# Where a gated ConvFFN convolves its five plain up-projection blocks

## The chip, the cores and the metric

The kernel runs on one core of a Trainium2 chip. The metric is device time in microseconds of one execution of the whole program. TensorE (PE) multiplies, ScalarE (ACT) and VectorE (DVE) do the elementwise work, GpSimd (POOL) helps with a few additions, and every DMA is issued by SyncE (SP), on one queue and in the order in which the program wrote it.

## The reference

One decoder layer over 2048 tokens of 1024 features: a token mixer, then the channel mixer that matters here. `causal_dwconv` is a three-tap convolution over positions with a bias, one set of taps for each of the 5632 features; the two features left of a position may come from the chunk before it.

```python
h = rms_norm(x, ln2_g[l]) * (1.0 + sc2) + sh2
u = jnp.einsum('bsd,df->bsf', h, w_up[l])
u = causal_dwconv(u, conv_w[l], conv_b[l])
a, v = jnp.split(u, 2, axis=-1)
x = x + gt2 * jnp.einsum('bsf,fd->bsd', jax.nn.silu(a) * v, w_down[l])
```

## The kernel before

The tokens are cut into four chunks of 512. Chunks 2p and 2p+1 form pass p, and each of the two passes runs the mixer for both chunks and then the FFN (`plan_ffn`). In the FFN the first chunk is called the first half (`m` = 0) and the second one the second half (`m` = 1). Every fp32 product is three matmuls over a high and a low part of both operands, so each weight and each activation is split: a cast on ACT gives the high part, a subtraction on DVE the low one (lines 129 and 132).

The up-projection has 22 blocks f of 128 gate features and 128 value features. Seventeen of them (5 to 21) go through a Strassen scheme over both halves at once, seven steps each (`strassen`). The first five are "plain": `plain(f, 0)` for f = 0 to 4 runs ahead of the Strassen blocks, while DVE and ACT build the operands of the scheme (`build("T1")` to `build("T4")`, `weights_first`), and `plain(f, 1)` for f = 0 to 4 runs behind them, just ahead of the down-projection. A plain block is 48 matmuls: 24 for the gate features, which fill one PSUM bank, and 24 for the value features, which fill another.

`conv_unit` (L1125 to L1144) takes a plain block's two banks. For each it scales on ACT (L1130), adds the two earlier taps on DVE (L1131, L1132), mends the first two columns from `halo` (L1134, L1135) and keeps the last two columns in it (L1136). Then come the Silu on ACT (L1139), the gate product on DVE (L1140) and, noted in `stores`, the write of that half of A[f] to DRAM. With `m` = 1 the first half of A[f] is read back (`fore`, L1151), since `diff_a` and `diff_b` need both halves for the operands of the down-projection.

A Strassen block does the same over 1024 columns: `open_ct` puts the halo ahead of them, `tap_act` (L1272) scales on ACT, `tap_vec` (L1280, L1281) adds two taps on DVE, `silu` (L1284) and `gate` (L1290) end it.

What sets the order: ACT and SP run in the program's order throughout. In the plain blocks DVE, PE and POOL are ordered by a planner; in the Strassen steps all five are in the program's order. `flush()` at the start of a block or step issues the stores that were noted before it, and a store waits on SP for the engine that makes its data. The weights of `plain(f, 1)` come back from DRAM as high and low parts (`w_load`, L1839), 2 MB a block, into four pairs of buffers and, while `big_pairs[0]` is 2, into two further pairs taken from the pool `big`, as soon as a block before has released them. `w_load()` stands at the end of a step, behind the step's own DMAs.

The down-projection is made of units of 18 or 15 matmuls. `unit(u)` issues the load of the weights of unit u+4, splits those of unit u+2 (`prep_w`, on ACT and DVE) and multiplies. Units 0 and 1 are split at the start of `plain(4, 1)`, ahead of its own work; the loads of units 0 to 3 stand there too.

Of the kernel before, what the change touches and what calls it, by code (L numbers as in the profile page):

```python
# [9 lines left out]
F32 = mybir.dt.float32  # L10
F32R = mybir.dt.float32r
U8 = mybir.dt.uint8
AF = mybir.ActivationFunctionType
# [4 lines left out]
P = 128  # L18
S = 2048
D = 1024  # L20
# [43 lines left out]
def kernel(  # L64
# [41 lines left out]
    def slot(dt=F32):  # L106
        return slots.tile([P, T], dt, tag="s", name="s")
# [238 lines left out]
    def at(i, fn):  # L346
        side[i].append(fn)
# [14 lines left out]
    def feature_mm(h, dst):  # L362
        def mm(w):
            pt = bank()
            n = 0
            for k in range(KD):
                if k == KD // 2:
                    run_half()
                for wv, hv in split_passes(w[0], h[k]):
                    pe.matmul(  # L370
                        pt, lhsT=wv[:, k * P : (k + 1) * P], rhs=hv, start=(n == 0), stop=(n == 3 * KD - 1)
                    )
                    n += 1
            dst.append(pt)

        return mm
# [140 lines left out]
    x1_d = [[dram.tile([P, D], F32, name=f"x1d{s}_{k}") for k in range(4)] for s in range(NSUB)]  # L517
    acts_d = [[dram.tile([P, D], F32, name=f"actd{i}_{f}") for f in range(NF)] for i in range(2)]
    T_d = [[[dram.tile([P, T], F32, name=f"td{i}_{t}_{p}") for p in range(NF // 2)] for t in range(4)] for i in range(2)]
    h12_d = [[dram.tile([P, T], F32, name=f"h12d{i}_{k}") for k in range(4)] for i in range(2)]  # L520

    def x1_of(s, j):
        return x1[s][j % 4][:, (j // 4) * T : (j // 4 + 1) * T]
# [583 lines left out]
    def plan_ffn(sg):  # L1107
# [11 lines left out]
        def taps(idx):  # L1119
            return [cw_sb[:, idx, j : j + 1] for j in range(3)]  # L1120

        fore = {}


        def conv_unit(f, m, pa, pv):  # L1125
            res = []
            for idx, pt in ((f, pa), (NF + f, pv)):
                t_ = slot()
                w0, w1, w2 = taps(idx)
                act.activation(t_, pt, AF.Identity, scale=w2, bias=cb_sb[:, idx : idx + 1])  # L1130
                vec.scalar_tensor_tensor(t_[:, 1:T], pt[:, 0 : T - 1], w1, t_[:, 1:T], op0=ALU.mult, op1=ALU.add)  # L1131
                vec.scalar_tensor_tensor(t_[:, 2:T], pt[:, 0 : T - 2], w0, t_[:, 2:T], op0=ALU.mult, op1=ALU.add)  # L1132
                hl = halo[:, idx, :]
                vec.scalar_tensor_tensor(t_[:, 0:1], hl[:, 1:2], w1, t_[:, 0:1], op0=ALU.mult, op1=ALU.add)  # L1134
                vec.scalar_tensor_tensor(t_[:, 0:2], hl, w0, t_[:, 0:2], op0=ALU.mult, op1=ALU.add)  # L1135
                vec.tensor_copy(hl, pt[:, T - 2 : T])  # L1136
                res.append(t_)
            ta, tv = res
            act.activation(ta, ta, AF.Silu)  # L1139
            vec.tensor_tensor(ta, ta, tv, op=ALU.mult)  # L1140
            stores.append((A[f][:, m * T : (m + 1) * T], ta))
            if m:
                made[f] = fore.pop(f), ta, tv

        def plain(f, m):
            def mm(w):
                flush()
                if m:
                    load_partner(f)
                    fore[f] = slot()  # L1150
                    sp.dma_start(fore[f], A[f][:, 0:T])  # L1151
                    for g in list(made):
                        diff_a(g)
                        diff_b(g)
                pts = []
                for wi in range(2):
                    feature_mm(h1T[(s0, s1)[m]], pts)([w[wi]])
                    while between:
                        between.pop()()
                conv_unit(f, m, *pts)  # L1160

            return mm


        def build(name):
            s0k = [x1_of(s0, k) for k in range(4)]
            spare = vec if sg else pool
            if name == "T1":
                h12 = [norm2_f32(s1, k) for k in range(4)]
                for k in range(4):  # L1170
                    sp.dma_start(h12_d[sg][k], h12[k])
                for k in range(4):
                    vec.tensor_tensor(s0k[k], h12[k], s0k[k], op=ALU.subtract)
                src = s0k
            elif name == "22":
                src = [norm2_f32(s1, k + 4) for k in range(4)]
            elif name == "T2":
                for k in range(4):
                    vec.tensor_tensor(s0k[k], x1_of(s1, k + 4), s0k[k], op=ALU.subtract)
                src = s0k  # L1180
            elif name == "T3":
                src = [x1_of(s1, k) for k in range(4)]
                for k in range(4):
                    spare.tensor_tensor(src[k], x1_of(s1, k + 4), src[k], op=ALU.subtract)
            else:
                src = [x1_of(s0, k + 4) for k in range(4)]
                for k in range(4):
                    spare.tensor_tensor(src[k], src[k], s0k[k], op=ALU.subtract)
            for k in range(4):
                B[name].append(parts_of(src[k]))  # L1190
            if name == "T4":
                B["11"] = [h1T[s0][k] for k in range(4)]
                B["21"] = [h1T[s0][k + 4] for k in range(4)]
                del x1[s0], x1[s1]
# [67 lines left out]
        def open_ct(f, c):  # L1262
            ct[c, f] = big()
            act.copy(ct[c, f][:, 0:2], halo[:, f + c * NF, :])

        def save_halo(f, c):
            act.copy(halo[:, f + c * NF, :], ct[c, f][:, D : D + 2])

        def tap_act(f, c):
            idx = f + c * NF  # L1270
            cvt[c, f] = big()
            act.activation(  # L1272
                cvt[c, f][:, 0:D], ct[c, f][:, 2 : 2 + D], AF.Identity, scale=taps(idx)[2], bias=cb_sb[:, idx : idx + 1]
            )

        def tap_vec(f, c):
            t_ = cvt[c, f][:, 0:D]
            src = ct.pop((c, f))
            w0, w1, _ = taps(f + c * NF)
            vec.scalar_tensor_tensor(t_, src[:, 1 : 1 + D], w1, t_, op0=ALU.mult, op1=ALU.add)  # L1280
            vec.scalar_tensor_tensor(t_, src[:, 0:D], w0, t_, op0=ALU.mult, op1=ALU.add)  # L1281

        def silu(f):
            act.activation(cvt[0, f][:, 0:D], cvt[0, f][:, 0:D], AF.Silu)  # L1284
# [3 lines left out]
        def gate(f):  # L1288
            a, v = cvt.pop((0, f))[:, 0:D], cvt.pop((1, f))[:, 0:D]
            vec.tensor_tensor(a, a, v, op=ALU.mult)  # L1290
            stores.append((A[f], a))
            made[f] = a[:, 0:T], a[:, T:D], v[:, 0:T]
# [199 lines left out]
            strassen(f, near(-1), near(1), near(2), near(-2))  # L1492
        add([], lambda: last_block(SF[-1]), "own")
        i1 = len(steps)
        for f in range(FILL):
            add([f"ua{f}", f"uv{f}"], plain(f, 1))

# [584 lines left out]
```

## Time and profile before

| | us |
|---|---|
| median of 3 runs | 2350.69 |
| lowest, highest | 2350.02, 2354.12 |
| profiled execution, its own time | 2356.09 |
| its span, first to last instruction | 2354.0 |
| TensorE busy in the span | 2291.7 |

All rows come from the profiled execution. Times are counted from the start of its span. A name such as `s<-ps` tells what an instruction writes and reads, and L1130 is line 1130 of the kernel. What stands in brackets with an arrow is the idle time of the engine ahead of an instruction and what ended it.

### The profile page before, as it was taken

How to read it: one execution, taken by the hardware profiler on the slowest of the kernel's cores; microseconds unless marked ns; L12 is line 12 of the kernel's file. 1: busy time of each engine (PE TensorE's matmuls, PEld its weight loads, DVE VectorE, ACT ScalarE, POOL GpSimd, SP SyncE). 2: the span in 40 equal slices, each digit the busy share in tenths (PEclk: the TensorE clock that was granted, in tenths of full speed). 3: DMA queues.
4: the chain of work that ended last, by engine and by line, in shares of the span. 5: the costliest groups of instructions: out<-in, count | busy, mean ns of one | idle time of the engine just before them, and what ended most of it. 6: DMA issues, size and time to landing. Idle time of an engine off the chain costs nothing. (4 is left out here: it accounts for less than half of the span.)

```text
span 2354.0 us, 32995 instructions
## 1 busy us (share of the span) xinstructions
PE 2291.7 (97%) x12310; PEld 1904.2 (81%) x12310; DVE 1672.2 (71%) x2641; ACT 1050.9 (45%) x1957; POOL 333.0 (14%) x320
## 2 busy tenths in 40 slices
PE   8999999998999999999999999999999999999996
PEld 6878788886888888788778888888888888888885
DVE  6677646658887788777894474446487788877778
ACT  5643433245555554443544242323455554535453
POOL 3342224112000000100134212320100000000001
PEclk9999999999999999999999999999999999999998
DMA  9866684647322237996664446344632223599751
GB/s 349 339 228 220 250 324 171 216 179 268 117 103 95 102 120 260 372 361 229 201 256 170 180 162 234 144 180 144 237 118 97 99 94 113 202 372 371 254 185 72
DMA packets 192639, 481.75 MB, mean 205 GB/s; under 512 B 21288, under 2 KB 36056, under 8 KB 192480
## 3 DMA queue, kind: packets, MB, share of 16 engines
q1 hardware_dynamic: 192480, 479.66, 56.6%
q8 instruction: 96, 1.57, 0.3%
q14 instruction: 63, 0.52, 0.1%
HBM read 366.20 MB, written 113.38 MB: 204 GB/s over the span
## 5 line engine op out<-in xcount | busy, mean ns | idle before, releaser
L1235 PE MATMUL ps<-s,whi 128*128 128x512 f32 x1904 | 586.2, 389 | 1.0 <-ACT whi L1224 1.0
L1235 PEld LDWEIGHTS ps<-s,whi 128*128 128x128 f32 x1904 | 357.2, 188 | 76.1 <-ACT whi L1224 1.4
L1567 PE MATMUL ps<-s,whi 128*128 128x512 f32 (+1 forms) x1272 | 386.8, 386 | 6.3 <-ACT whi L129 3.3
L1235 PE MATMUL ps<-s,wlo 128*128 128x512 f32 x952 | 369.8, 389 | 0.0
L370 PE MATMUL ps<-s,whi 128*128 128x512 f32 x1040 | 325.5, 395 | 10.8 <-ACT whi L129 10.8
L462 POOL TENSOR_TENSOR s<-s 128x512 f32<-128x512 f32 (+1 forms) x69 | 96.7, 1402 | 1490.3 <-ACT s L461 955.9
L1567 PEld LDWEIGHTS ps<-s,whi 128*128 128x128 f32 x1272 | 239.3, 190 | 55.9 <-DVE s L132 4.7
L858 PE MATMUL ps<-whi,s 128*128 128x512 f32 (+1 forms) x992 | 252.6, 345 | 0.0
L1567 PE MATMUL ps<-s,wlo 128*128 128x512 f32 (+1 forms) x636 | 245.4, 387 | 4.9 <-DVE wlo L132 4.9
L370 PEld LDWEIGHTS ps<-s,whi 128*128 128x128 f32 x1040 | 194.4, 189 | 53.3 <-ACT whi L129 12.0
L132 DVE TENSOR_TENSOR wlo<-big,whi 128x768 fp32r<-128x768 f32 (+3 forms) x152 | 161.8, 1070 | 73.7 <-ACT whi L129 71.8
L1235 PEld LDWEIGHTS ps<-s,wlo 128*128 128x128 f32 x952 | 178.7, 188 | 36.9
L370 PE MATMUL ps<-s,wlo 128*128 128x512 f32 x520 | 203.4, 392 | 1.5 <-DVE wlo L132 1.5
L370 PE MATMUL ps<-s,big 128*128 128x512 f32 x792 | 185.6, 391 | 0.0
L858 PEld LDWEIGHTS ps<-whi,s 128*128 128x128 f32 x992 | 165.2, 189 | 20.9 <-issue 0.4
L129 ACT CAST whi<-big 128x768 fp32r<-128x768 f32 (+3 forms) x160 | 134.5, 848 | 106.5 <-DVE big L1548 26.3
L370 PEld LDWEIGHTS ps<-s,big 128*128 128x128 f32 x792 | 147.8, 188 | 31.7 <-issue 1.3
L858 PE MATMUL ps<-wlo,s 128*128 128x512 f32 (+2 forms) x496 | 150.3, 341 | 3.1 <-DVE wlo L132 3.1
L1228 DVE TENSOR_TENSOR wlo<-big,whi 128x1024 fp32r<-128x1024 f32 (+1 forms) x136 | 145.4, 1085 | 5.9 <-ACT whi L1224 5.7
L1224 ACT CAST whi<-big 128x1024 fp32r<-128x1024 f32 (+1 forms) x136 | 127.6, 940 | 41.4 <-DVE big L1212 41.4
L1567 PEld LDWEIGHTS ps<-s,wlo 128*128 128x128 f32 x636 | 120.9, 190 | 29.9 <-DVE wlo L132 6.7
L1280 DVE SCALAR_TENSOR_TENSOR big<-big,cw_sb 128x1024 f32<-128x1024 f32 x68 | 87.4, 1285 | 68.2 <-ACT big L1272 68.2
(228 smaller groups left out, 3652.1 us busy)
## 6 DMA issues: line engine op xcount, KB each, us to landing
big<-in_wt SPq DMA_DIRECT2D x104, 512.0 KB, 3.3
s<-td SPq DMA_DIRECT2D x110, 256.0 KB, 5.1
big<-in_wd SPq DMA_DIRECT2D x72, 384.0 KB, 6.3
s<-actd SPq DMA_DIRECT2D x98, 256.0 KB, 5.3
s<-in_w_ada SPq DMA_DIRECT2D x96, 256.0 KB, 6.0
big<-in_wd SPq DMA_DIRECT2D x72, 320.0 KB, 4.2
actd<-big SPq DMA_DIRECT2D x34, 512.0 KB, 2.6
td<-s SPq DMA_DIRECT2D x54, 256.0 KB, 5.5
```

The source lines that it names most:

```text
L129: act.copy(hi, src)
L132: (lo_engine or vec).tensor_tensor(lo, src, hi.bitcast(F32), op=ALU.subtract)
L370: pe.matmul(pt, lhsT=wv[:, k * P : (k + 1) * P], rhs=hv, start=(n == 0), stop=(n == 3 * KD - 1))
L462: engine.tensor_tensor(acc, acc, sq, op=ALU.add)
L858: pe.matmul(pt[:, 0 : c1 - c0], lhsT=hv[:, tt * P : (tt + 1) * P], rhs=wv[:, k2 * stride + c0 : k2 * stride + c1], start=(m == 0), stop=(m ...
L1224: act.copy(dst[f][0][:, 0:n], src[f][:, 0:n])
L1228: vec.tensor_tensor(lo[:, 0:n], src[f][:, 0:n], hi[:, 0:n].bitcast(F32), op=ALU.subtract)
L1235: pe.matmul(pt, lhsT=wv[:, c0 : c0 + P], rhs=hv, start=(start and n == 0), stop=(n == 11), skip_group_check=not start)
L1280: vec.scalar_tensor_tensor(t_, src[:, 1 : 1 + D], w1, t_, op0=ALU.mult, op1=ALU.add)
L1567: pe.matmul(pt[:, cols], lhsT=wv[:, ki * P : (ki + 1) * P], rhs=hv[:, cols], start=(start and n == 0), stop=(n == 3 * np_ - 1), skip_group ...
```

## The change

With `m` = 0 a plain block no longer convolves. Its two banks are copied on ACT to two buffers, and these raw products are stored to DRAM (`raw_d`, 256 KB each). With `m` = 1 the two raw halves are read back into the left halves of two `ct` buffers, the new products are copied beside them, and the block is convolved over 1024 columns with the Strassen blocks' own helpers. One store then writes all of A[f], 512 KB, and `fore` is gone.

Two smaller edits go with it. In pass 0 the eight subtractions of `build("T3")` and `build("T4")` move from POOL to DVE, where pass 1 already had them. And `big_pairs[0]` is set to 0 at the start of the second half's plain blocks, so that no further weight pair goes into the pool `big`.

```diff
@@ -517,6 +517,7 @@
     x1_d = [[dram.tile([P, D], F32, name=f"x1d{s}_{k}") for k in range(4)] for s in range(NSUB)]
     acts_d = [[dram.tile([P, D], F32, name=f"actd{i}_{f}") for f in range(NF)] for i in range(2)]
     T_d = [[[dram.tile([P, T], F32, name=f"td{i}_{t}_{p}") for p in range(NF // 2)] for t in range(4)] for i in range(2)]
+    raw_d = [[[dram.tile([P, T], F32, name=f"rawd{i}_{f}_{c}") for c in range(2)] for f in range(FILL)] for i in range(2)]
     h12_d = [[dram.tile([P, T], F32, name=f"h12d{i}_{k}") for k in range(4)] for i in range(2)]
 
     def x1_of(s, j):
@@ -1119,52 +1120,42 @@
         def taps(idx):
             return [cw_sb[:, idx, j : j + 1] for j in range(3)]
 
-        fore = {}
-
-
-        def conv_unit(f, m, pa, pv):
-            res = []
-            for idx, pt in ((f, pa), (NF + f, pv)):
-                t_ = slot()
-                w0, w1, w2 = taps(idx)
-                act.activation(t_, pt, AF.Identity, scale=w2, bias=cb_sb[:, idx : idx + 1])
-                vec.scalar_tensor_tensor(t_[:, 1:T], pt[:, 0 : T - 1], w1, t_[:, 1:T], op0=ALU.mult, op1=ALU.add)
-                vec.scalar_tensor_tensor(t_[:, 2:T], pt[:, 0 : T - 2], w0, t_[:, 2:T], op0=ALU.mult, op1=ALU.add)
-                hl = halo[:, idx, :]
-                vec.scalar_tensor_tensor(t_[:, 0:1], hl[:, 1:2], w1, t_[:, 0:1], op0=ALU.mult, op1=ALU.add)
-                vec.scalar_tensor_tensor(t_[:, 0:2], hl, w0, t_[:, 0:2], op0=ALU.mult, op1=ALU.add)
-                vec.tensor_copy(hl, pt[:, T - 2 : T])
-                res.append(t_)
-            ta, tv = res
-            act.activation(ta, ta, AF.Silu)
-            vec.tensor_tensor(ta, ta, tv, op=ALU.mult)
-            stores.append((A[f][:, m * T : (m + 1) * T], ta))
-            if m:
-                made[f] = fore.pop(f), ta, tv
 
         def plain(f, m):
             def mm(w):
                 flush()
                 if m:
                     load_partner(f)
-                    fore[f] = slot()
-                    sp.dma_start(fore[f], A[f][:, 0:T])
+                    for c in range(2):
+                        open_ct(f, c)
+                        sp.dma_start(ct[c, f][:, 2 : 2 + T], raw_d[sg][f][c])
                     for g in list(made):
                         diff_a(g)
                         diff_b(g)
-                pts = []
-                for wi in range(2):
-                    feature_mm(h1T[(s0, s1)[m]], pts)([w[wi]])
+                for c in range(2):
+                    pts = []
+                    feature_mm(h1T[(s0, s1)[m]], pts)([w[c]])
                     while between:
                         between.pop()()
-                conv_unit(f, m, *pts)
+                    if m == 0:
+                        t_ = slot()
+                        act.copy(t_, pts[0])
+                        stores.append((raw_d[sg][f][c], t_))
+                        continue
+                    act.copy(ct[c, f][:, 2 + T : 2 + D], pts[0])
+                    tap_act(f, c)
+                    save_halo(f, c)
+                    tap_vec(f, c)
+                    if c == 0:
+                        silu(f)
+                    else:
+                        gate(f)
 
             return mm
 
 
         def build(name):
             s0k = [x1_of(s0, k) for k in range(4)]
-            spare = vec if sg else pool
             if name == "T1":
                 h12 = [norm2_f32(s1, k) for k in range(4)]
                 for k in range(4):
@@ -1181,11 +1172,11 @@
             elif name == "T3":
                 src = [x1_of(s1, k) for k in range(4)]
                 for k in range(4):
-                    spare.tensor_tensor(src[k], x1_of(s1, k + 4), src[k], op=ALU.subtract)
+                    vec.tensor_tensor(src[k], x1_of(s1, k + 4), src[k], op=ALU.subtract)
             else:
                 src = [x1_of(s0, k + 4) for k in range(4)]
                 for k in range(4):
-                    spare.tensor_tensor(src[k], src[k], s0k[k], op=ALU.subtract)
+                    vec.tensor_tensor(src[k], src[k], s0k[k], op=ALU.subtract)
             for k in range(4):
                 B[name].append(parts_of(src[k]))
             if name == "T4":
@@ -1492,6 +1483,7 @@
             strassen(f, near(-1), near(1), near(2), near(-2))
         add([], lambda: last_block(SF[-1]), "own")
         i1 = len(steps)
+        at(i1, lambda: big_pairs.__setitem__(0, 0))
         for f in range(FILL):
             add([f"ua{f}", f"uv{f}"], plain(f, 1))
 
```

## Rows read from the trace of the kernel before

**Rows 1.** Page, busy time: us, share of the span, instructions of each engine.

```profile
PE 2291.7 (97%) x12310; PEld 1904.2 (81%) x12310; DVE 1672.2 (71%) x2641; ACT 1050.9 (45%) x1957; POOL 333.0 (14%) x320
```

**Rows 2.** Busy time by stretch (from:to length, busy each, PEclk, DMA): the plain blocks.

```profile
core 0: us, PE busy (x) PEld busy (x) DVE busy (x) ACT busy (x) POOL busy (x), PEclk, DMA share, GB/s
536.60:603.70 67.10, 57.27 (x240) 46.56 (x239) 61.25 (x97) 40.11 (x58) 14.17 (x8) 0.90 0.72 264
1682.70:1738.10 55.40, 54.39 (x241) 44.69 (x239) 48.80 (x98) 33.07 (x51) 0.00 (x0) 1.00 0.55 187
927.50:982.00 54.50, 54.39 (x240) 44.70 (x239) 39.20 (x72) 19.64 (x31) 10.07 (x7) 1.00 1.00 366
2062.30:2116.70 54.40, 54.40 (x242) 45.05 (x241) 39.18 (x77) 16.90 (x26) 0.00 (x0) 1.00 1.00 368
```

**Rows 3.** Timeline (start, length, instruction) of PE: the gap in pass 0's first half.

```profile
589.60 2.17 PE L370 MATMUL ps<-s,whi 128*128 128x512 f32 x4 [9.83 <-ACT whi L129]
```

**Rows 4.** Timeline of ACT ahead of that matmul.

```profile
579.44 1.44 ACT L1130 ACTIVATE s<-ps,cb_sb,cw_sb 128x512 f32<-128x512 f32 x2
587.99 0.63 ACT L1139 ACTIVATE s<-s 128x512 f32<-128x512 f32 x1 [7.10 <-DVE s L1135]
588.52 1.03 ACT L129 CAST whi<-big 128x1024 fp32r<-128x1024 f32 x1
```

**Rows 5.** Views of lines 1179 and 1184: ns min/median/max, first and last start.

```profile
L1179 DVE TENSOR_TENSOR big<-big x8: 684/1230/1782, 570.3 to 1714.6; 128x512 f32<-128x512 f32 x8
L1184 DVE TENSOR_TENSOR big<-big x4: 683/685/686, 1715.8 to 1719.4; 128x512 f32<-128x512 f32 x4
```

**Rows 6.** Groups by shape: count, busy us, mean ns | idle time before, releasers.

```profile
L1131 DVE SCALAR_TENSOR_TENSOR s<-ps,cw_sb,s 128x511 f32<-128x511 f32 x40 | 29.8, 745 | 7.2 <-ACT s L1130 7.2
L1338 ACT COPY big<-ps 128x512 f32<-128x512 f32 x34 | 19.9, 586 | 22.1 <-PE ps L1235 22.1
L1272 ACT ACTIVATE big<-big,cb_sb,cw_sb 128x1024 f32<-128x1024 f32 x68 | 84.6, 1245 | 5.0 <-DVE big L1332 3.8
L1280 DVE SCALAR_TENSOR_TENSOR big<-big,cw_sb 128x1024 f32<-128x1024 f32 x68 | 87.4, 1285 | 68.2 <-ACT big L1272 68.2
L1284 ACT ACTIVATE big<-big 128x1024 f32<-128x1024 f32 x34 | 36.1, 1062 | 23.5 <-DVE big L1281 23.5
L1290 DVE TENSOR_TENSOR big<-big 128x1024 f32<-128x1024 f32 x34 | 41.5, 1219 | 0.0
```

**Rows 7.** Waits of SP's queue: us in total, times, longest.

```profile
SPq L1117 <- DVE big L1290: 246.6, 30, 10.7
```

**Rows 8.** Timeline of SP in pass 1's first second-half block.

```profile
2071.59 0.32 SPq L1117 DMA_DIRECT2D actd<-big  x1
...
2073.70 0.45 SPq L1151 DMA_DIRECT2D s<-actd  x1
```

**Rows 9.** View of line 1151: its ten DMAs from issue to landing.

```profile
DMA to landing us min/median/max: 4.6/5.9/7.1
```

**Rows 10.** The same row for all DMAs of tile actd.

```profile
DMA to landing us min/median/max: 2.0/5.1/9.5
```

**Rows 11.** Timelines of PE, ACT and DVE where pass 1's down-projection starts.

```profile
2116.45 0.62 PE L1567 MATMUL ps<-s,whi 128*128 128x512 f32 x2
...
2118.04 1.28 ACT L119 ACT_TABLE_LOAD   x1
2119.34 0.84 ACT L129 CAST whi<-big 128x768 fp32r<-128x768 f32 x1
...
2120.20 0.96 DVE L132 TENSOR_TENSOR wlo<-big,whi 128x768 fp32r<-128x768 f32 x1
```

**Rows 12.** Timelines of DVE and PE in pass 0's second half.

```profile
949.33 0.69 DVE L1312 TENSOR_TENSOR s<-s 128x512 f32<-128x512 f32 x1 [5.16 <-DMA s<-actd]
...
983.93 0.73 PE L1567 MATMUL ps<-s,whi 128*128 128x512 f32 x2 [2.04 <-ACT whi L129]
```

**Rows 13.** Page, DMA issues: count, KB each, median us to landing.

```profile
big<-in_wd SPq DMA_DIRECT2D x72, 384.0 KB, 6.3
```

## The prediction, made before the change was run

> **What bounds the kernel now.** The page's first part comes first: TensorE is busy for 2291.7 us of a span of 2354.0 [rows 1]. The change removes no matmul, so all it can win is idle PE time, 62 us in the whole kernel, and only what of it lies in the plain blocks. The busy times by stretch show that [rows 2]. Five plain blocks are 240 matmuls. In both second halves, and in pass 1's first half but for one microsecond, PE is busy throughout, and 240 matmuls take 54.4 us: 10.9 us a block, 0.227 us a matmul. In pass 0's first half they take 67.1 us, 12.7 more, at a granted clock of 0.90. The PE timeline says where: one gap of 9.83 us, ended by a cast on ACT [rows 3]; the other 2.9 us are the slow clock behind it (the lower of the two levels, 1.2 GHz). The ACT timeline gives the cause [rows 4]: the cast of the next block's weights stands in program order behind the Silu of a convolution, and the Silu waited 7.10 us for DVE. DVE is busy for 61.25 of the 67.1 us [rows 2]. The second halves are the opposite: DVE is busy for 39 of 54 us, but the DMA engines have a share of 1.00 at 366 to 368 GB/s [rows 2]. So the change takes work from a stretch bound by DVE and ACT's order, and puts work, loads and stores into one bound by the DMA queue.
>
> **First halves: the gain.** Each block loses four taps of 0.745 us on DVE, 3.0 us, and its halo columns and gate product besides [rows 6]: over 15 us a pass. ACT gets two copies of 0.586 us [rows 6] and no Silu, so nothing on it waits for a convolution. The eight subtractions moved in pass 0 add 8 x 0.685 = 5.5 us to DVE [rows 5]; but DVE's own subtractions of that size take up to 1.782 us there, and 0.684 at best [rows 5], while POOL runs its slow ones, and that goes too. DVE keeps 61.25 - 15 + 5.5 = 52 us at most, and less by the slowed ones, over 54.4 us, and PE needs the results only at the cast, one block ahead. Next late would be T4 and the first Strassen weights; they have the last block to hide in. I take the whole excess: 12.7 us in pass 0 and 1.0 in pass 1, 13.7 us. Were the gap to stay, 0; more than 13.7 isn't there to win. The stores grow from one of 256 KB to two a block; DMA has a share of 0.55 to 0.72 there [rows 2], and they wait for ACT copies alone.
>
> **Second halves: a new loop.** The kernel before needs its read-back only for the differences, so a late one holds up nothing on PE. In the changed kernel a raw half is needed by `tap_act`, and `tap_act` stands on ACT ahead of everything later. The order on SP in block f is: flush the store of A[f-1], which waits for `gate(f-1)` on DVE; two partner loads; the two raw loads; then the weights of block f+2. That SP really stands still at such stores is shown by the Strassen blocks' waits: 246.6 us in 30 waits for the same gate product [rows 7]. So `gate(f-1)` releases raw(f), raw(f) releases `tap_act(f)`, and that leads to `gate(f)`: a chain of its own, block by block, beside PE.
>
> Its period. (a) From the gate to the issue of the first raw load, three steps on SP of 0.45 us: 1.4 us; they took 2.1 us in the full queue [rows 8]. (b) To landing: the loads that the raw ones replace took 4.6 to 7.1 us, 5.9 in the middle [rows 9]; all loads and stores of that tile go down to 2.0 [rows 10]. I take 4.6, since the queue drains while SP stands. (c) From landing to the gate, in ACT's program order (scale, taps, Silu, copy, scale, taps, gate): 1.245 + 2 x 1.285 + 1.062 + 0.586 + 1.245 + 2 x 1.285 + 1.219 = 10.5 us [rows 6]. Together 16.5 us against 10.9 us of matmuls. Bounds: 1.4 + 2.0 + 10.5 = 13.9 and 2.1 + 5.9 + 10.5 = 18.5. Even (c) alone nearly fills a block, so the chain falls behind in any case.
>
> The Trainium skill, page "DMA: Bandwidth & Descriptors", section "Anatomy of one DMA", prices a DMA at about 2.0 us plus its bytes over 436 GB/s, an estimate of 2.6 us for 256 KB. By that figure the period would be 14.5 us, and the sum below some 16 us less (2.0 us in four periods of two passes); the loads of this stretch have shown no such landing [rows 9]. The same section says that DMA engines don't wait on semaphores but the issuing sequencer does, before dispatch. This speaks against the change, and the waits of [rows 7] agree.
>
> **Pass 1, in times of the trace before.** raw(0) takes the place of the load at 2073.70 [rows 8] and lands at 2078.3. gate(0) is at 2088.8, gate(4) four periods later at 2154.8. Who waits for it? First the weights of blocks 3 and 4: with `big_pairs` at 0 they are loaded one block later, behind the raw loads, at 1.4 us for 512 KB [rows 2]; a few microseconds of stall each, which the later waits swallow. Then units 0 and 1, whose casts stand behind block 3's second scale. Then unit 2, whose cast stands behind block 4's second scale: two taps and a gate before gate(4), at 2151.0, plus a table load of 1.28, the cast of 0.84 and the low part of 0.96 [rows 11], so at 2154.1. Before, the down-projection began at 2116.45 [rows 11] and unit 2 two times 18 matmuls later, at 2124.6. That is 29.5 us lost. Unit 4's weights are loaded behind the store of A[4] and three difference stores: 2154.8 + 3 x 0.69 + 3 x 0.45 = 2158.2, landed after 6.3 us [rows 13] at 2164.5, split at 2166.3, while PE could have begun it at 2162.3. 4.0 us more; the slow clock behind the stall, 2.9 us as in the gap before, hides in it. Sum 33.5 us.
>
> **Pass 0.** The same, but raw(0) lands later: the first read-back let DVE go on at 949.33 [rows 12], 32.6 us ahead of the end of the stretch, against 38.2 us in pass 1. 5.6 us more; the 2.0 us that PE waited here before [rows 12] are no longer extra. 33.5 + 5.6 - 2.0 = 37.1 us.
>
> **Sum.** -13.7 + 33.5 + 37.1 = +57 us. Against the profiled execution that is 2356 + 57 = 2413 us; this execution lies 5.4 us above the median of the runs, so on the median it is 2350.7 + 57 = 2408 us. With the short period gate(4) comes 4 x 2.6 = 10.4 us sooner in each pass: 2387. With the long one it comes 4 x 2.0 + 1.3 = 9.3 us later: 2426. The bytes add 512 KB a block, 1.4 us at 367 GB/s; they are inside the chain, since the engines idle while SP stands.
>
> **Rivals.**
> A, faster: the chain stays clear of PE, because raw halves land before the block's first bank is full. Then the gain stands alone: 2350.7 - 13.7 = 2337 us. The deciding point is a period of 10.9 us or less. For it: the first halves' gap is certain, and PE has banks and weights for some blocks in hand. Against it: (c) alone is 10.5 us.
> B, no change: the chain is short, but the DMA queue is full, and 2.6 MB more a pass at 367 GB/s are 7.1 us each: -13.7 + 14.2, so 2351 us. For it: the share of 1.00 [rows 2]. Against it: the stretch gets longer by the chain, and the share falls.
> C, half the price: only units 0 and 1 wait, because unit 2's cast is reached early. Unit 0 needs 2138.3 - 3.8 + 0.84 + 0.96 = 2136.3, that is 19.9 us late, and 23.5 in pass 0: 2351 - 13.7 + 43 = 2380 us.
> D, the gap of the first half stays, since the eight subtractions keep DVE late: 12.7 us more than the forecast, 2421 us. DVE's 52 of 54 us speak a little for it.
>
> **How the numbers follow.** The chain as summed, with its bounds and D: 0.70; C: 0.13; A: 0.11; B: 0.06. The time is that of the chain, 2408 us. The range reaches from just below C, 2372, to the long period with some contention on top, 2432; it leaves out A, B and the edges of the rest, some 0.2. Faster by over 0.2% (some 5 us, about what a measurement of this kernel can tell from no change) has A and a share of B: 0.13; within 0.2%: 0.03; slower: 0.84.
>
> **What would show it.** In the changed profile: no gap before the cast in pass 0's first half, 240 matmuls in some 54.4 us in both first halves; in the second halves SP waiting at A's store for L1290's line in every block, gates about 16.5 us apart, `tap_act` on ACT waiting for a raw load, PE idle some 30 us a pass in pieces, the largest ahead of unit 0 and unit 2, at a lower granted clock, and a DMA share well below 1.00. Gates about 11 us apart would make it wrong, and so would PE running through blocks 3 and 4 and units 0 to 4 without a wait.

## The result, and the profile after

The changed kernel takes 2415.95 us (median of 4 runs, 2412.29 to 2418.21), the kernel before, run beside it, 2351.05 us (4 runs). The ratio is 1.0272, with a 95% interval of 1.0256 to 1.0289: 65 us slower, 8 us above the forecast.

The page of the changed kernel begins with the busy times; below them stand the same four stretches as in [rows 2]: both first halves cover the five plain blocks' 240 matmuls, both second halves run on into the down-projection.

```profile
PE 2311.2 (96%) x12310; PEld 1913.1 (79%) x12310; DVE 1650.1 (68%) x2479; ACT 1068.2 (44%) x2007; POOL 321.2 (13%) x312
```

```profile
536.00:590.10 54.10, 54.10 (x240) 44.78 (x239) 43.68 (x64) 34.75 (x53) 0.00 (x0) 1.00 0.90 343
1709.10:1763.40 54.30, 54.30 (x241) 44.91 (x240) 36.20 (x57) 28.59 (x46) 0.00 (x0) 1.00 0.61 216
913.80:1024.90 111.10, 80.51 (x301) 62.57 (x300) 64.31 (x65) 42.48 (x76) 11.61 (x7) 0.83 0.70 250
2087.10:2193.80 106.70, 80.92 (x313) 62.96 (x311) 58.42 (x64) 38.03 (x67) 0.00 (x0) 0.87 0.70 247
```

The same 12310 matmuls, and none is missing. The first halves are full: 240 matmuls in 54.1 us at a granted clock of 1.00, where pass 0 took 67.10 at 0.90 [rows 2]. The second halves are not: in pass 1, 106.7 us hold 80.9 us of PE work, at 0.87. Full speed would have done those 313 matmuls in 71.0 us (0.227 us each), so 25.8 us are idle time and 9.9 us slow clock.

Where each stretch begins in the two traces gives the whole account, with no matmul counted:

| begins | before [rows 2] | after | later by | gained or lost in the stretch before it |
|---|---|---|---|---|
| pass 0, first half | 536.6 | 536.0 | -0.6 | |
| pass 0, second half | 927.5 | 913.8 | -13.7 | -13.1 |
| pass 1, first half | 1682.7 | 1709.1 | +26.4 | +40.1 |
| pass 1, second half | 2062.3 | 2087.1 | +24.8 | -1.6 |
| end of the span | 2354.0 | 2416.5 | +62.5 | +37.7 |

(What lies between two plain stretches is in the figure of the earlier one.)

The first halves first. ACT's timeline in pass 0, to be set beside [rows 4]: the cast of the next weights stands behind two copies now and starts at 571.43, where the Silu held it until 588.52.

```profile
570.48 1.05 ACT L1142 COPY s<-ps 128x512 f32<-128x512 f32 x2
571.43 1.06 ACT L129 CAST whi<-big 128x1024 fp32r<-128x1024 f32 x1
```

In pass 1's second half, SP's timeline shows the new loop. Each store of A (`actd<-big`, 512 KB) waits for the gate product; the two raw loads of the next block follow it.

```profile
2096.68 0.32 SPq L1118 DMA_DIRECT2D actd<-big  x1
2098.66 1.04 SPq L1131 DMA_DIRECT2D big<-rawd  x2
...
2114.24 0.32 SPq L1118 DMA_DIRECT2D actd<-big  x1
2115.90 0.92 SPq L1131 DMA_DIRECT2D big<-rawd  x2
...
2131.68 0.32 SPq L1118 DMA_DIRECT2D actd<-big  x1
2133.29 0.96 SPq L1131 DMA_DIRECT2D big<-rawd  x2
...
2149.27 0.32 SPq L1118 DMA_DIRECT2D actd<-big  x1
2150.93 0.90 SPq L1131 DMA_DIRECT2D big<-rawd  x2
...
2167.41 0.32 SPq L1118 DMA_DIRECT2D actd<-big  x1
2169.02 0.98 SPq L1131 DMA_DIRECT2D big<-rawd  x2
...
2185.86 0.32 SPq L1118 DMA_DIRECT2D actd<-big  x1
```

The stores of A[0] to A[4], from 2114.24 to 2185.86, are 17.4, 17.6, 18.1 and 18.5 us apart; a block's matmuls take 10.9. ACT's timeline of block 1 has the rest of the loop:

```profile
2121.03 1.24 ACT L1263 ACTIVATE big<-big,cb_sb,cw_sb 128x1024 f32<-128x1024 f32 x1 [9.96 <-issue]
...
2124.95 1.06 ACT L1275 ACTIVATE big<-big 128x1024 f32<-128x1024 f32 x1 [2.59 <-DVE big L1272]
2125.91 0.57 ACT L1145 COPY big<-ps 128x512 f32<-128x512 f32 x1
2126.51 1.24 ACT L1263 ACTIVATE big<-big,cb_sb,cw_sb 128x1024 f32<-128x1024 f32 x1
```

A[0] stored at 2114.24, the load issued 1.66 us later at 2115.90, the first scale 5.13 us after that at 2121.03, the store of A[1] 10.65 us after that at 2131.68. The Silu waits 2.59 us for DVE's taps, with the copy and the second scale queued behind it. The waits by releaser say the same of the whole kernel: SP for the gate product, which was 246.6 us in 30 waits [rows 7], and ACT for the raw loads (columns: us in total, times, longest).

```profile
SPq L1118 <- DVE big L1281: 339.4, 39, 14.7
...
ACT big L1263 <- DMA big<-rawd: 66.6, 7, 14.6
```

The view of L1131, the raw loads, has their time from issue to landing:

```profile
DMA to landing us min/median/max: 4.8/5.2/5.5
```

And PE's timeline of that half, the lines with a wait of over 1 us:

```profile
2122.91 1.22 PE L370 MATMUL ps<-s,whi 128*128 128x512 f32 x2 [2.97 <-DMA whi<-wpua]
...
2140.85 0.70 PE L370 MATMUL ps<-s,whi 128*128 128x512 f32 x2 [3.83 <-DMA whi<-wpua]
...
2163.61 1.22 PE L1559 MATMUL ps<-s,whi 128*128 128x512 f32 x2 [9.23 <-ACT whi L129]
...
2166.31 0.80 PE L1559 MATMUL ps<-s,wlo 128*128 128x512 f32 x1 [1.47 <-DVE wlo L132]
...
2183.47 1.22 PE L1559 MATMUL ps<-s,whi 128*128 128x512 f32 x2 [7.58 <-ACT whi L129]
```

They are the weights of blocks 3 and 4, unit 0 (high and low part) and unit 2, 25.1 us in sum. Pass 0 has the same five, 30.1 us in sum: 9.16, 3.38, 10.30, 1.47 and 5.79 us.

### The profile page after: what moved, and what is told of

Same layout as the page of the kernel before. It is cut to its first block, busy times and chain, and to the rows that moved or that the text cites. A ratio compares the mean times of both kernels' runs of the same rounds, so it can differ in the third digit from the quotient of the medians.

```text
span 2416.5 us, 32923 instructions
## 1 busy us (share of the span) xinstructions
PE 2311.2 (96%) x12310; PEld 1913.1 (79%) x12310; DVE 1650.1 (68%) x2479; ACT 1068.2 (44%) x2007; POOL 321.2 (13%) x312
## 4 chain that ended last, share of the span: by engine, by line
PE 75%; DVE 10%; issue 5%; DMA 4%; ACT 4%; POOL 1%; SPq 1%; DVEq 0%; ACTq 0%; POOLq 0%
PE ps L1226 26%; PE ps L370 15%; PE ps L1559 13%; PE ps L859 12%; PE ps L894 3%; DVE wlo L132 1%; DMA big<-rawd 1%; PE ps L716 1%; PE ps L717 1%; ACT big L1263 1%; DVE big L1271 1%; DVE big L1272 1%; PE ps L690 1%; DVE s L1673 1%; DVE s L132 1%
## 5 line engine op out<-in xcount | busy, mean ns | idle before, releaser
L1226 PE MATMUL ps<-s,whi 128*128 128x512 f32 x1904 | 586.2, 389 | 0.0
L1559 PE MATMUL ps<-s,whi 128*128 128x512 f32 (+1 forms) x1272 | 394.5, 392 | 37.3 <-ACT whi L129 34.1
L1226 PEld LDWEIGHTS ps<-s,whi 128*128 128x128 f32 x1904 | 357.2, 188 | 74.5 <-DVE big L1326 0.5
L370 PE MATMUL ps<-s,whi 128*128 128x512 f32 x1104 | 351.5, 400 | 20.3 <-DMA whi<-wpua 19.3
L1226 PE MATMUL ps<-s,wlo 128*128 128x512 f32 x952 | 370.0, 389 | 0.0
L1559 PEld LDWEIGHTS ps<-s,whi 128*128 128x128 f32 x1272 | 243.4, 194 | 90.4 <-ACT whi L129 36.6
L370 PEld LDWEIGHTS ps<-s,whi 128*128 128x128 f32 x1104 | 210.3, 193 | 67.4 <-DMA whi<-wpua 13.0
L370 PE MATMUL ps<-s,wlo 128*128 128x512 f32 x552 | 220.1, 399 | 2.5 <-DVE wlo L132 1.5
L1271 DVE SCALAR_TENSOR_TENSOR big<-big,cw_sb 128x1024 f32<-128x1024 f32 x88 | 113.0, 1284 | 153.0 <-ACT big L1263 147.4
L129 ACT CAST whi<-big 128x768 fp32r<-128x768 f32 (+3 forms) x160 | 134.5, 848 | 103.6 <-PE ps L1559 26.4
L370 PE MATMUL ps<-s,big 128*128 128x512 f32 x696 | 163.5, 391 | 0.0
L1263 ACT ACTIVATE big<-big,cb_sb,cw_sb 128x1024 f32<-128x1024 f32 x88 | 109.5, 1244 | 100.5 <-DMA big<-rawd 66.6
L370 PEld LDWEIGHTS ps<-s,big 128*128 128x128 f32 x696 | 129.7, 188 | 28.0 <-issue 1.3
```

Source lines behind the costliest of these rows:

```text
L129: act.copy(hi, src)
L370: pe.matmul(pt, lhsT=wv[:, k * P : (k + 1) * P], rhs=hv, start=(n == 0), stop=(n == 3 * KD - 1))
L1226: pe.matmul(pt, lhsT=wv[:, c0 : c0 + P], rhs=hv, start=(start and n == 0), stop=(n == 11), skip_group_check=not start)
L1263: act.activation(cvt[c, f][:, 0:D], ct[c, f][:, 2 : 2 + D], AF.Identity, scale=taps(idx)[2], bias=cb_sb[:, idx : idx + 1])
L1559: pe.matmul(pt[:, cols], lhsT=wv[:, ki * P : (ki + 1) * P], rhs=hv[:, cols], start=(start and n == 0), stop=(n == 3 * np_ - 1), skip_group ...
```

## Experiments

What each tells apart: the first three shorten or cut the loop; the next takes away the weights' stalls; then the bytes alone; then three on the first half's gap; the last two ask what is left of the gain. Each is compared with the kernel before, run on the same chip (medians 2352.2 to 2352.9).

### The raw loads ahead of the store

```diff
             def mm(w):
-                flush()
                 if m:
-                    load_partner(f)
                     for c in range(2):
                         open_ct(f, c)
                         sp.dma_start(ct[c, f][:, 2 : 2 + T], raw_d[sg][f][c])
+                flush()
+                if m:
+                    load_partner(f)
```

> The changed kernel, but in the second half's plain blocks the two raw loads stand on SP ahead of flush(), so ahead of the store of A[f-1]. Theory (the chain gate(f-1), store, raw(f), scale, gate(f)): raw(f) now follows gate(f-2), so the chain has two blocks of matmuls, 21.8 us, for one period of 17.5 us, and PE is nearly undisturbed: 2416 - 77 + some 10 for pass 0's late first load, so 2340 to 2358 us. Rival (the queue is full, the bytes cost): the same loads in another order cost the same, 2410 to 2420 us.

Measured: 2373.89 us, ratio 1.0095 (1.0080 to 1.0110). Two thirds of the loss are gone, so the loop through SP made them; but the time isn't the one expected. SP's timeline says why:

```profile
2089.04 0.32 SPq L1118 DMA_DIRECT2D actd<-big  x1
...
2092.89 4.57 SPq L1512 DMA_DIRECT2D s<-actd  x6
2098.83 1.54 SPq L1129 DMA_DIRECT2D big<-rawd  x2
...
2116.80 0.32 SPq L1118 DMA_DIRECT2D actd<-big  x1
```

The loop isn't cut, it has become a loop over two blocks. A[0]'s store at 2089.04 still stands ahead of raw(2) on SP, and so do two partner loads, four weight loads and six operand loads (L1512): raw(2) is issued at 2098.83 and A[2] stored at 2116.80, 27.8 us for two blocks, 13.9 for one. The four periods from A[0] to A[4] take 55.0 us, after 71.6 in the changed kernel, and A[0] is stored 12.8 us after the store ahead of it instead of 17.6. That is 21.4 us a pass, 43 in both; the loss fell from 65 to 22 us, by 43. So the loop's length is passed on to PE one for one. (The 21.4 us are read in pass 1; in pass 0 the same count gives 22.)

### The Silu behind the second scale

```diff
                     tap_vec(f, c)
-                    if c == 0:
+                    if c == 1:
                         silu(f)
-                    else:
                         gate(f)
```

> The changed kernel, but the Silu stands behind the second scale on ACT, so that the value half's scale no longer waits for the gate half's taps. Theory: the part from landing to gate shrinks from 10.6 us to 1.24 + 2.6 + 2.6 + 1.2 = 7.7 us, the period from 17.5 to 14.6 us, and unit 2 starts some 13.6 us sooner in each pass: 2416 - 27 = 2389 us, 2383 to 2396. Rival (bytes): nothing on the queue has moved, 2413 to 2419 us.

Measured: 2388.05 us, ratio 1.0154 (1.0132 to 1.0175), as the loop said. ACT's and SP's timelines of block 0:

```profile
2085.98 1.24 ACT L1262 ACTIVATE big<-big,cb_sb,cw_sb 128x1024 f32<-128x1024 f32 x1 [9.99 <-DMA big<-rawd]
...
2087.82 1.25 ACT L1262 ACTIVATE big<-big,cb_sb,cw_sb 128x1024 f32<-128x1024 f32 x1
...
2089.89 1.06 ACT L1274 ACTIVATE big<-big 128x1024 f32<-128x1024 f32 x1 [0.76 <-DVE big L1271]
```

```profile
2093.74 0.32 SPq L1118 DMA_DIRECT2D actd<-big  x1
```

From the first scale to the store of A[0] it takes 7.8 us; in the changed kernel block 0 took 10.65, as block 1 did. The second scale no longer stands behind a Silu that waits for the taps. The four periods from A[0] to A[4] take 59.3 us, 12.3 less, and A[0] is stored 14.4 us after the store ahead of it instead of 17.6. That is 15.4 us a pass, 31 in both; the loss fell by 29. No byte and no operation differs from the changed kernel.

### Raw loads a block further ahead, Silu late

```diff
+                if m:
+                    for g in ((0, 1) if f == 0 else (f + 1,)):
+                        for c in range(2):
+                            if g < FILL:
+                                ct[c, g] = big()
+                                sp.dma_start(ct[c, g][:, 2 : 2 + T], raw_d[sg][g][c])
+                    for c in range(2):
+                        act.copy(ct[c, f][:, 0:2], halo[:, f + c * NF, :])
                 flush()
                 if m:
                     load_partner(f)
-                    for c in range(2):
-                        open_ct(f, c)
-                        sp.dma_start(ct[c, f][:, 2 : 2 + T], raw_d[sg][f][c])
...
-                    if c == 0:
+                    if c == 1:
                         silu(f)
-                    else:
                         gate(f)
```

> The changed kernel with both knots of the chain undone: the raw loads of block f+1 are issued in block f ahead of flush() (those of blocks 0 and 1 in block 0), and the Silu stands behind the second scale. Same instructions, same bytes as the changed kernel, and eight more us of lead for a load. Theory (order, not work, costs): nearly the whole loss goes, 2416 - 77 + 5 = 2344 us, 2338 to 2354. Rival (the bytes and the longer DVE work of the second half cost by themselves): 2365 us or more.

Measured: 2351.69 us, ratio 1.0001 (0.9990 to 1.0012). With the same work and the same bytes the whole loss against the kernel before is gone: the loop made it. But the time is that of the kernel before, not 13.7 us below it, though the first halves keep their gain. Counted between the begins of the stretches, as in the table above, the first halves are 14.4 us shorter than in the kernel before, and the second halves 8.9 us longer in pass 0 and 5.3 in pass 1. PE's and ACT's timelines of pass 1 show what is late there:

```profile
2110.98 0.83 ACT L129 CAST whi<-big 128x768 fp32r<-128x768 f32 x1 [8.19 <-DMA big<-in_wd]
```

```profile
2111.86 0.78 PE L1563 MATMUL ps<-s,whi 128*128 128x512 f32 x2 [2.91 <-ACT whi L129]
```

Now unit 0's weights land late. ACT waits 8.19 us for them and PE 2.91. In pass 0 PE waits 3.11 us for the same, and 2.82 us for the weights of a plain block. These waits, with the slow clock behind them, are the part that can be named.

### Weight pairs in the big pool kept

```diff
-        at(i1, lambda: big_pairs.__setitem__(0, 0))
```

> The changed kernel, with big_pairs[0] left at 2 in the second half, so that the weights of blocks 3 and 4 are loaded a block earlier again. Theory (the later waits of the chain swallow the earlier ones): the stalls ahead of blocks 3 and 4 go (9.2, 3.4 and 3.0, 3.8 us in the changed kernel), PE waits as much longer ahead of unit 0, and the time stays: 2412 to 2420 us. Rival (the stalls add up): 2393 to 2400 us.

Measured: 2415.95 us, ratio 1.0265 (1.0246 to 1.0283): no difference from the changed kernel. PE's timeline of pass 1 has no wait ahead of blocks 3 and 4 any more, and

```profile
2163.57 1.22 PE L1558 MATMUL ps<-s,whi 128*128 128x512 f32 x2 [22.29 <-ACT whi L129]
```

unit 0 starts at 2163.57, where the changed kernel had 2163.61. What PE doesn't lose at the weights it loses at unit 0. The weights' stalls were swallowed, as the prediction said.

### The kernel before with the bytes alone

The block loads its half of A[f] a second time and stores it to a place that nobody reads: 512 KB more a block, and nothing more for any engine to compute.

```diff
+    extra_d = dram.tile([P, T], F32, name="extrad")
...
                     fore[f] = slot()
                     sp.dma_start(fore[f], A[f][:, 0:T])
+                    more = slot()
+                    sp.dma_start(more, A[f][:, 0:T])
+                    stores.append((extra_d, more))
```

> The kernel before, with one more load of 256 KB and one more store of 256 KB in each second-half block (the bytes that the change adds there), which nobody waits for. Theory: the queue's own price is a few us at most, 2351 to 2357 us. Rival (the full queue passes on its 7.1 us a pass): 2365 us.

Measured: 2370.86 us, ratio 1.0081 (1.0065 to 1.0097), 18 us more. I had expected next to nothing; the rival that prices the bytes was nearer. ACT's and PE's timelines in pass 1:

```profile
2127.73 1.77 ACT L129 CAST whi<-big 128x768 fp32r<-128x768 f32 x2 [10.12 <-DMA big<-in_wd]
```

```profile
2128.61 1.22 PE L1571 MATMUL ps<-s,whi 128*128 128x512 f32 x2 [5.86 <-ACT whi L129]
```

PE waits 5.86 us ahead of unit 0, where it didn't wait before, and 10.30 in pass 0, where it waited 2.04 [rows 12]: 14.1 us more, about the 2 x 7.1 of rival B; the rest is slow clock behind the two gaps and what I can't place. The caveat: the extra store waits on SP until the extra load has landed, so a part may be the queue standing there (the DMA share of the stretch is 0.95, not 1.00).

### The kernel before, with the subtractions moved to DVE

```diff
-            spare = vec if sg else pool
+            spare = vec
```

> The kernel before, with the eight subtractions of T3 and T4 of pass 0 on DVE, nothing else. Theory (the convolutions make DVE late in pass 0's first half): DVE still has 61 - 7 + 5.5 = 60 us of work for 54 us, so most of the 9.8 us gap stays: 2345 to 2351 us. Rival (POOL slows DVE's subtractions, and that alone makes the gap): the gap goes, 2338 to 2341 us.

Measured: 2347.45 us (10 runs), ratio 0.9979 (0.9970 to 0.9988). PE's and ACT's timelines in pass 0's first half:

```profile
579.44 1.74 PE L370 MATMUL ps<-s,whi 128*128 128x512 f32 x3 [5.48 <-ACT whi L129]
```

```profile
577.82 0.63 ACT L1139 ACTIVATE s<-s 128x512 f32<-128x512 f32 x1 [7.33 <-DVE s L1135]
```

The gap of 9.83 us [rows 3] falls to 5.48, and the Silu still waits 7.33 us for the taps. So this small edit alone takes 4 us of the gap. What is left of it still stands behind the waiting Silu; whether the Silu's place makes it is asked two experiments further on.

### The changed kernel, with the subtractions kept on POOL

```diff
-                    vec.tensor_tensor(src[k], x1_of(s1, k + 4), src[k], op=ALU.subtract)
+                    spare.tensor_tensor(src[k], x1_of(s1, k + 4), src[k], op=ALU.subtract)
...
-                    vec.tensor_tensor(src[k], src[k], s0k[k], op=ALU.subtract)
+                    spare.tensor_tensor(src[k], src[k], s0k[k], op=ALU.subtract)
```

Here `spare` is POOL in pass 0, as before the change.

> The changed kernel, with the eight subtractions of pass 0 left on POOL. Theory (convolutions): the gap of the first half stays closed or comes back with 3 us at most, since no Silu stands ahead of the cast: 2415 to 2420 us. Rival (POOL makes the gap): 10 to 13 us come back, 2426 to 2430 us.

Measured: 2422.81 us, ratio 1.0304 (1.0287 to 1.0322): 7 us more than the changed kernel, between the two expectations. PE's timeline has a gap although no Silu stands in the way:

```profile
585.18 0.50 PE L370 MATMUL ps<-s,wlo 128*128 128x512 f32 x1 [3.50 <-DVE wlo L132]
```

and ACT's shows the cause one step earlier, casts that wait for DVE's subtractions (L1171, up to 1782 ns each, as in [rows 5]):

```profile
577.61 0.62 ACT L129 CAST s<-big 128x512 fp32r<-128x512 f32 x1 [2.77 <-DVE big L1171]
```

So the first half's gap had two causes at least, which overlap: the Silu order on ACT, and DVE slowed beside POOL. Either one alone leaves a gap.

### The kernel before, with the first half's Silu a block later

```diff
-            act.activation(ta, ta, AF.Silu)
-            vec.tensor_tensor(ta, ta, tv, op=ALU.mult)
-            stores.append((A[f][:, m * T : (m + 1) * T], ta))
+            def end():
+                act.activation(ta, ta, AF.Silu)
+                vec.tensor_tensor(ta, ta, tv, op=ALU.mult)
+                stores.append((A[f][:, m * T : (m + 1) * T], ta))
...
+            if m or f == FILL - 1:
+                end()
+            else:
+                ends.append(end)
...
                 flush()
+                while ends:
+                    ends.pop(0)()
...
-            spare = vec if sg else pool
+            spare = vec
```

> The kernel before, with the first half's Silu and gate product of blocks 0 to 3 put one block later in the program, and the eight subtractions of pass 0 on DVE; convolutions as before. Theory (the 9.83 us gap is a cast that stands behind a Silu on ACT): the gap goes without any change of where it is convolved, 2351 - 12.7 = 2338 us, 2335 to 2342. Rival (DVE simply has too much to do in that stretch): a gap of 4 us or more stays, 2343 to 2350.

Measured: 2344.92 us (6 runs), ratio 0.9968 (0.9955 to 0.9981), 8 us of the 13 expected: the rival's range, and its gap of 4 us or more. The cast is on time now, but PE waits for the low part of the same weights:

```profile
583.31 0.50 PE L370 MATMUL ps<-s,wlo 128*128 128x512 f32 x1 [4.35 <-DVE wlo L132]
```

On DVE that subtraction stands behind the taps of the convolution (L1131, L1132) and starts at 582.04. With the taps in the first half, DVE's order takes the place of ACT's; that leaves 4.35 us of the 5.48 that moving the subtractions alone had left. Of the runs here, only those with the taps out of the first half and the subtractions on DVE have no gap. Another order on DVE was not tried.

### Weights ahead of the operands, with the loop cut

On top of the raw loads a block further ahead and the late Silu, the weight pairs are kept, and the loads of the weights of units 0 to 3 stand ahead of the operand loads:

```diff
-        at(i1, lambda: big_pairs.__setitem__(0, 0))
...
-        at(i1 + 4, lambda: load_op(0, "P2"))
         at(i1 + 3, lambda: [split_op(0, "P1", n) for n in range(DOWN_PAIRS[0])])
         at(i1 + 4, lambda: [load_w(u) for u in range(W_LOAD)])
+        at(i1 + 4, lambda: load_op(0, "P2"))
```

> The kernel of e7 (raw loads two blocks ahead, Silu behind the second scale), with the weights of units 0 to 3 loaded ahead of the six operands of P2, which are needed later, and with the further weight pairs kept. Theory (what e7 still loses is the added bytes' 7 us a pass, passed on through the loads that unit 0 and blocks 3 and 4 wait for): six loads of 0.7 us less ahead of unit 0's weights take 3 to 4 us a pass, and the pairs 3 to 4 us in pass 0: 2352 - 10 = 2342 us, 2337 to 2346. Rival (another cause holds unit 0): 2350 us or more.

Measured: 2347.48 us (12 runs), ratio 0.9980 (0.9971 to 0.9988). That is 1.5 us above the range that I expected. The two edits together give 4 us; what each gives was not measured. The waits that went are the 2.82 us for a plain block's weights in pass 0 and the 2.91 us for unit 0 in pass 1. In pass 0 PE still waits 3.83 us for unit 0, in pass 1 2.3 us at unit 2. Five of the 13.7 us stay.

### The same order in the kernel before

The late first Silu, the subtractions on DVE and the order of the loads just shown, with the convolution as before:

```diff
-        at(i1 + 4, lambda: load_op(0, "P2"))
         at(i1 + 3, lambda: [split_op(0, "P1", n) for n in range(DOWN_PAIRS[0])])
         at(i1 + 4, lambda: [load_w(u) for u in range(W_LOAD)])
+        at(i1 + 4, lambda: load_op(0, "P2"))
```

> The kernel of e8 (convolution as before the change, Silu of the first half one block later, subtractions on DVE), with the weights of units 0 to 3 loaded ahead of the six operands of P2. Theory: pass 0's wait of 2 us ahead of unit 0 and its slow clock go: 2345 - 4 = 2341 us, 2338 to 2345. Rival: unit 0's weights are not what is late, and the time stays at 2345.

Measured: 2343.50 us (5 runs), ratio 0.9964 (0.9952 to 0.9976). It has the lowest median of all, 9 us below the kernel before, though its interval overlaps that of the run with the late first Silu, so the order of the loads is not shown to add anything here. There is no wait ahead of unit 0, and in the first half the wait for the low part stays (4.42 us). The part of the gain that costs no byte is the better part.

## Why the prediction was right, step by step

**What bounds the kernel.** TensorE's idle time was the thing to count, and the account of the result closes in it.

**First halves, -12.7 and -1.0.** Measured -13.1 and -1.6. The gap went as a whole. The stated cause, the cast behind the waiting Silu, was only part of it: with the Silu out of the way and POOL kept on the subtractions, 3.5 us of gap stay, with the subtractions moved and the Silu kept, 5.48, and with both mended but the taps still there, 4.35. The prediction had counted the slowed subtractions only as room on DVE. The whole gap went because the change takes away the Silu, the taps and POOL's subtractions together. The prediction named all three but made the Silu the cause; that the size came out all the same is in part luck. Rival D fell: DVE is busy for 43.7 us of the first stretch, below the 52 that I took as the most.

**The loop.** Gate, store, raw load, scale, gate is there as it was drawn, SP standing at the store in each block. The experiments that shorten it take the time back about one for one (21.4 and 15.4 us a pass, against 43 and 29 us in all), and the one that cuts it takes back all. That it is the cause is shown.

**The period, 16.5 us.** This was the mis-sized term: 17.4 to 18.5. In block 1 the three parts are 1.66, 5.13 and 10.65, after 1.4, 4.6 and 10.5. There the landing is the main error, but not in the four periods together, which are 5.6 us too long. The issues make 0.9 us of that, the landings (5.13, 4.38, 5.10 and 5.45 from the issue to the first scale) 1.7, and the last part (10.65, 11.60, 11.38 and 11.39) 3.0. The sum of that part had left out DVE's other work: in blocks 2 to 4 subtractions that split the operands and the weights of the units stand ahead of the gate (two of 0.68 us in block 2, one of 0.95 us in blocks 3 and 4). ACT's first scale of block 2, and DVE's subtractions and gate there:

```profile
2137.67 1.24 ACT L1263 ACTIVATE big<-big,cb_sb,cw_sb 128x1024 f32<-128x1024 f32 x1 [9.17 <-issue]
```

```profile
2145.62 0.68 DVE L132 TENSOR_TENSOR s<-s 128x512 fp32r<-128x512 f32 x1
...
2147.42 0.68 DVE L132 TENSOR_TENSOR s<-s 128x512 fp32r<-128x512 f32 x1
2148.02 1.22 DVE L1281 TENSOR_TENSOR big<-big 128x1024 f32<-128x1024 f32 x1
```

For the landing I took the lower end of [rows 9], since the queue would drain while SP stands. In the period ahead of A[1] the DMA share (the last figure but one of the window) is 0.94, so the queue hadn't drained:

```profile
2114.20:2131.60 17.40, 14.41 (x51) 10.94 (x50) 8.32 (x9) 4.84 (x9) 0.00 (x0) 0.80 0.94 343
```

The Trainium skill, page "DMA: Bandwidth & Descriptors", section "Anatomy of one DMA", was the source of the 2.6 us for the landing; its fit is for DMAs issued by GpSimd, which the prediction didn't say, and these are issued by SP. By the view of L1131 none of the 20 raw loads was under 4.8 us, so the measurement decides here. (Block 2's scale began 4.38 us after the issue, so that view and the timeline agree to some 0.4 us only.)

**Unit 2, 29.5 us late.** It starts at 2183.47; with the 24.8 us by which the half itself begins later, and 2124.6 before, that is 34.1 us. Block 0 came 0.6 us later than forecast, and the three periods that unit 2 waits for were 53.2 us instead of 49.5; these make 4.3 of the 4.6 us. PE began on the cast alone, so the 0.96 us that the sum had added for the low part hid most of block 4's late landing. What releases unit 2 was right, the table load and the cast behind block 4's second scale:

```profile
2181.29 1.28 ACT L119 ACT_TABLE_LOAD   x1
2182.58 0.83 ACT L129 CAST whi<-big 128x768 fp32r<-128x768 f32 x1
```

**Unit 4, 4.0 us, with the slow clock hidden in it.** Two errors that cancel. Its weights are loaded at 2189.55 and cast at 2192.93, as SP's and ACT's timelines show, 3.4 us later and not 6.3 [rows 13]; a few microseconds ahead of that load the DMA share was 0.00. So unit 4 waits next to nothing.

```profile
2189.55 0.89 SPq L1529 DMA_DIRECT2D big<-in_wd  x2
```

```profile
2192.93 0.83 ACT L129 CAST whi<-big 128x768 fp32r<-128x768 f32 x1 [6.25 <-DMA big<-in_wd]
```

The clock behind unit 2's stall, though, is no longer covered. A window, whose last three figures are the granted clock, the DMA share and GB/s:

```profile
2183.50:2186.50 3.00, 2.93 (x6) 1.93 (x7) 3.00 (x5) 3.00 (x6) 0.00 (x0) 0.50 0.00 0
```

Behind the stall PE runs at the lower of its two levels, 1.2 GHz. From unit 2 to the end 37.7 - 34.1 = 3.6 us are added, where I had 4.0. Of these, some 2 us lie ahead of unit 4, which starts at 2193.82, 10.35 us after unit 2; two units at full speed take 8.2. The rest was not traced.

**Pass sums.** 33.5 became 37.7 and 37.1 became 40.1. Pass 1's excess is the period. Pass 0 has the same periods (17.3 to 18.4 us), and by these and by A[0], stored 1.2 us later than forecast, its unit 2 should come 5.3 us late. It came 2.5 us late. Most of the difference lies in the kernel before: its units 0 and 1 took 10.4 us there instead of 8.2, at a granted clock of 0.84 behind the wait of 2.04 us [rows 12]. The forecast had taken off the wait and not this slow stretch:

```profile
983.90:994.30 10.40, 10.11 (x36) 7.97 (x37) 9.99 (x19) 7.71 (x11) 0.00 (x0) 0.84 0.96 368
```

In sum 62.5 us of span after a forecast of 57.

**The bytes "inside the chain".** In the changed kernel they are, since PE waits for the loop and the DMA share is 0.70. That they cost nothing was wrong as a general remark: with the loop gone weights come late, and the second halves stay 14.2 us longer than before the change. Rival B had forecast 14.2 for the bytes, and its 2351 us would have been the result with the raw loads a block further ahead and the Silu late: 2351.7 measured in that experiment. That the bytes make all of these 14.2 us is not shown; the run that adds bytes alone lost 18 us, with the caveat given there.

**The other rivals.** A asked for a period of at most 10.9 us, and the loop's last part alone took 10.65; even with the loop cut, no order of the loads that was tried gave its 2337 us. C fell with unit 2's wait of 7.58 us.

## What to carry to other kernels

When a value that was only passed through memory becomes an operand, follow the new loop through every queue that issues in order: a store that waits for an engine holds back the loads behind it, and their landing and the consumer's chain make a period. Put every other instruction that its engines run in between into the period, and compare it with the matmul time of one round; what it exceeds is paid on TensorE, as here, whatever the busy shares say. And ask separately what the same bytes cost where the queue is already full, since curing the loop brings that price out.

## What the runs showed of the hardware

A DVE subtraction of 128x512 takes 0.684 us alone, and up to 1.782 while POOL runs its own subtractions [rows 5]. In the changed kernel, with POOL out, the same eight, which are line 1170 there, run in 0.682 to 0.693:

```profile
L1170 DVE TENSOR_TENSOR big<-big x8: 682/685/693, 565.8 to 1735.2; 128x512 f32<-128x512 f32 x8
```

The Trainium skill, page "SBUF — State Buffer", section "Who interferes with whom", says that a DVE instruction with two SBUF inputs contends with a GpSimd instruction that reads SBUF. These rows agree that the two contend (what is held, and for how long, they don't show), and the experiment that moves the subtractions alone gives the price here, 5 us.

How long a load took followed what was in the queue more than its size: the raw loads of 256 KB landed in 4.8 to 5.5 us, unit 4's weights of 384 KB within 3.4 us, right after the DMA engines had stood still. A median over a kernel is a poor price for a load that follows a stall.
